# A hybrid attention and convolution block: x's first half loaded ahead of the modulation weights, zero products at the start, one store on another queue

## The chip, the cores and the metric

One Trainium2 chip, of which the kernel uses one core. The metric is the device time of one execution in microseconds (us); the time of a kernel is the median of its runs.

## What is computed

The reference, cut to the parts that the changed stage works on:

```python
def rmsnorm(x, g):                       # over the 1024 features
    y = x * lax.rsqrt(jnp.mean(x * x, axis=-1, keepdims=True) + 1e-6)
    return y * g

def adaln(cond, w_ada, b_ada):           # w_ada: 1024 x 3072
    return jnp.split(jax.nn.silu(cond) @ w_ada + b_ada, 3, axis=-1)

def hybrid_layer(x, ctx, c, c_ctx, ...):
    shift, scale, gate = adaln(c, w_ada, b_ada)
    shift_c, scale_c, gate_c = adaln(c_ctx, w_ada, b_ada)
    h = rmsnorm(x, norm_g) * (1 + scale[:, None]) + shift[:, None]
    hc = rmsnorm(ctx, norm_g) * (1 + scale_c) + shift_c
    q, k, v, za, u, bg, cg, zc = jnp.split(h @ w_in, SPLIT_POINTS, axis=-1)
    ...                                  # QK-norm, axial rope on q and k, windowed attention with
                                         # a bias table and context keys; gated short convolution
    return x + gate[:, None] * (jnp.concatenate([attn, conv], axis=-1) @ w_out)
```

`x` is 1024 tokens by 1024 features, `ctx` is 256 tokens, `w_in` is 1024 x 4096, all in float32. The conditioning vectors `c` and `c_ctx` give a shift and a scale per feature; they come out of a product of two rows with `w_ada`.

## The kernel before

Large products are made with three TensorE passes each: an operand is split into a high part (float32r) and a rest, and high x high, high x rest and rest x high are added up (`mm3`, and written out in `first_columns`).

The stage that the diff touches is the first one. It makes `h` transposed, feature tile by feature tile: `hh[k]` and `hl[k]` are the high part and the rest of 128 features by 1024 tokens. At the same time it uses each feature tile at once for the first convolution group: three blocks of 128 columns of `w_in` (a chunk, `chunks[k]`) times `hh[k]` and `hl[k]`, added up over the eight feature tiles in six PSUM banks `acc0[u][half]` (`first_columns(half, k, part)`, where a part is one of the three passes: part 0 needs the chunk's high part `wh`, part 1 its rest `wl`, part 2 the rest of `h`). A half is 512 tokens, four tiles of 128: `xx[0]` to `xx[3]` and `xx[4]` to `xx[7]`.

The steps for a tile of x: `square` (ScalarE, with the sum over the row), `root` (VectorE adds the epsilon, GpSimd takes the power -0.5 of the 128 sums), `norm` (VectorE scales the tile in place). Then for a half and a feature tile: `transposed` (TensorE, four transposes into a PSUM bank) and `turn`: ScalarE writes the modulated high part `h`, VectorE or ScalarE the full value `hw`, VectorE the rest of `h`.

The steps for the shifts and scales: slabs of `w_ada` are loaded, 256 columns for the shift (`j = 0`) and 256 for the scale (`j = 1`), so that pair `m` serves the feature tiles `2m` and `2m + 1`. `products(m, j)` multiplies the two activated conditioning vectors (two columns of weights) with the slab over eight tiles of 128 rows, in plain float32 for `m < 2`, where every product leaves two matmul records in the trace. `row_copy` brings the result rows to SBUF, and `modulation` turns them by tiny products into a column per feature tile, which VectorE completes in `ab`. From `m = 2` on the slab is split into `slabh` and `slabl` first.

In the trace the PSUM tile of slabs and transposes is called `tr`, that of `first_columns` `acc`, a tile of x `xx`, its sums `xss`, a chunk `wr` (`wh` and `wl` when split). Nearly all instructions have line 55, since the wrapper class `ordered` records them.

The order of the work is written out by hand. While `strict` holds the engines, each instruction of TensorE, ScalarE, VectorE and GpSimd is tied behind the one before it in program order, and the loads that SP issues too. A DMA that another engine than SP issues isn't tied. So an engine that waits holds up all that is written behind it, and so does SP: a load whose buffer isn't free yet, or a store whose data isn't ready, keeps all later transfers waiting.

The order of the loads before: both slabs of pair 0 (in two parts of 512 KB each), four tiles of x, a chunk, four tiles of x, a chunk, and then the slabs and chunks that follow as buffers come free (slabs of pairs 1 to 3 share three buffers, chunks five). Later, in the loop over `m` from 1 to 3, GpSimd makes the rope tables `rg` in `gains`, and SP stores them to `rope_d`, from where the next stage loads them; behind this store SP issues the chunks of the next column group (`chunk_load(CQ, k)`), then the small copies that build the bias tables (`bias_tables`, `t_d` in the trace), and then the first loads of the next stage (`uraw`, a unit of weights for the convolution and gates). The next stage makes q, k and v tile by tile (`pacc`): ScalarE and VectorE normalize and rotate a tile (`qn`, `rot`), and TensorE transposes it (`trA`, `trB`). All four engines go on through attention and the output projection, which the diff doesn't touch.

Of the kernel before, what the change touches and what calls it, by code (L numbers as in the profile page):

```python
# [19 lines left out]
P = 128  # L20
# [19 lines left out]
def body(tc, es, x, ctxt, w_ada, b_ada, w_in, q_g, k_g, rpbr, w_out, vecs, cst, out):  # L40
# [100 lines left out]
    def place(k, shape, dtype, name):  # L141

        return hpool.tile(shape, dtype, name=name, tag=f"h{k}")
# [383 lines left out]
    def load_x(ts):  # L527
        for t in ts:
            xx[t] = xp.tile([P, D], F32, name="xx", tag="xx", bufs=8)
            sp.dma_start(xx[t], x[0, t * P:(t + 1) * P])  # L530

    def load_slab(m, j):

        new = place(6 + j, [P, KT, 256], F32, "slab") if m == 0 else sl.tile([P, KT, 256], F32, name="slab", tag="slab", bufs=3)
        n = 2 if m == 0 else 1
        for i in range(n):
            rows = slice(KT // n * i, KT // n * (i + 1))
            sp.dma_start(new[:, rows], bass.AP(w_ada.tensor, w_ada.offset + j * D + 256 * m + 3 * D * P * rows.start,
                                               [[3 * D, P], [3 * D * P, KT // n], [1, 256]]))
        slabs[m, j] = new  # L540

    def load_chunks(ks):
        for k in ks:
            chunks[k] = chunk_load(CU, k)

    load_slab(0, 0)
    load_slab(0, 1)
    load_x(range(4))
    load_chunks([0])
    load_x(range(4, 8))  # L550
    load_chunks([1])
    load_slab(1, 0)
    load_slab(1, 1)
    load_chunks([2, 3])
# [3 lines left out]
    for u, half in (0, 0), (2, 0), (0, 1), (2, 1), (1, 0), (1, 1):  # L558
        acc0[u][half] = ps0.tile([P, 512], F32, name=f"acc{u}{half}", tag=f"acc{u}{half}")

    pv = tr()
    pe.transpose(pv[:, :nvec], vec[:nvec], ident[:nvec, :nvec])
    dve.tensor_copy(vecT, pv[:, :nvec])
    act.activation(c2[:].rearrange("p k a -> p a k"), vecT[:, 0:16].rearrange("p (a k) -> p a k", a=2), AF.Silu)
    dve.tensor_scalar(b1, bsc, 1.0, None, ALU.add)
    c4 = cp.tile([P, KT, 4], F32R, name="c4")
    act.copy(c4[:, :, 0:2], c2)
    dve.tensor_tensor(c4[:, :, 2:4], c2, c4[:, :, 0:2].bitcast(F32), ALU.subtract)

    sums = {}  # L570
# [34 lines left out]
    def row_copy(m):  # L605
        n = 2 if m < 2 else 4
        rw = cvp.tile([4, 512], F32, name="rw", tag="ub", bufs=2)
        act.copy(rw[:n], mods[m][:n])
        return rw[:n]

    def modulation(m, rw):

# [77 lines left out]
    def gains(tables):  # L690

        rw, gqk = tables
        pool.tensor_scalar(gqk[:, 0], gqk[:, 0], 0.125, None, ALU.mult)
        gkc1 = cp.tile([P, 1, HD], F32, name="gkc")
        pool.tensor_tensor(gkc1[:, 0], gqk[:, 0], gqk[:, 1], ALU.mult)
        rg = sl.tile([P, 2, NB, 2, HD], F32, name="rg", tag="slab", bufs=3)
        for n in range(2):
            rraw = rw[:, 512 * n:512 * n + 512].rearrange("p (b d) -> p b d", d=HD)
            for k in range(2):
                pool.tensor_tensor(rg[:, n, :, k], rraw, gqk[:, k:k + 1].broadcast_to([P, NB, HD]), ALU.mult)  # L700
        sp.dma_start(rope_d, rg[:].rearrange("p n b k d -> p (n b k d)"))
        return gkc1[:]

    def bias_tables():
# [10 lines left out]

    more_h(range(6))

    products(0, 0)
    products(0, 1)
    for t in range(4):  # L720
        square(xx[t], t)
    root(0)
    root(1)
    norm(xx[0], 0)
    root(2)
    norm(xx[1], 1)
    root(3)
    norm(xx[2], 2)
    rw = row_copy(0)
    modulation(0, rw)  # L730
    norm(xx[3], 3)
    transposed(0, 0)
    transposed(0, 1)
    square(xx[4], 4)
    root(4)
    split_chunk(0)
    turn(0, 0, dve)
    square(xx[5], 5)
    norm(xx[4], 4)
    root(5)  # L740
    turn(0, 1, dve)
    first_columns(0, 0)
    square(xx[6], 6)
    norm(xx[5], 5)
    root(6)
    square(xx[7], 7)
    norm(xx[6], 6)
    root(7)
    split_chunk(1)
    norm(xx[7], 7)  # L750
    first_columns(0, 1)
    products(1, 0, range(4))
    transposed(1, 0)
    turn(1, 0, act)
# [668 lines left out]
```

## Time and profile before

| | |
|---|---|
| median of 3 runs | 651.97 us (651.77 to 652.3) |
| the profiled execution | 651.68 us |
| its span, first to last instruction | 649.9 us |
| mean granted TensorE clock | 0.994 |
| TensorE busy with matmuls | 629.0 us (97%), 3469 |
| TensorE weight loads | 539.2 us (83%) |
| VectorE | 431.9 us (66%) |
| ScalarE | 322.6 us (50%) |
| GpSimd | 129.4 us (20%) |
| DMA | 125.46 MB, mean 193 GB/s |

PE is TensorE, PEld its weight loads, ACT is ScalarE, DVE is VectorE, POOL is GpSimd, SP is SyncE, which issues most transfers; PEq, SPq and the like are an engine's own queue of instructions. A line of the timeline has the start, the length, the engine, the source line, the operation with the tiles that it writes and reads and its shape, the count of merged instructions, and in brackets the idle time ahead of it with what ended that. Lengths of matmuls are modelled and overlap; the distance from one start to the next is the better measure. A line of the windows has the stretch, its length, the busy time and count of TensorE, its weight loads, VectorE, ScalarE and GpSimd, then the granted clock, the DMA engines' share and GB/s.

### The profile page before, as it was taken

The numbers are of one execution on the slowest core, as the hardware profiler recorded it, in microseconds if no ns is written. First come the engines' busy times: TensorE is split into PE (matmuls) and PEld (weight loads), VectorE is DVE, ScalarE is ACT, GpSimd is POOL, SyncE is SP. The second block draws the span as 40 slices with busy tenths as digits, with TensorE's granted clock in tenths as the row PEclk, the third lists the DMA queues.
The fourth block names the chain that finished last, engine by engine and source line by source line (L and its number), as shares of the span: only waits on it lengthen the run. The fifth ranks groups of instructions, "written<-read, shape, count | busy, mean of one in ns | idle before, by whom it ended". The sixth has DMA issues, their size and how long they took to land.

```text
span 649.9 us, 10273 instructions
## 1 busy us (share of the span) xinstructions
PE 629.0 (97%) x3469; PEld 539.2 (83%) x3469; DVE 431.9 (66%) x814; ACT 322.6 (50%) x693; POOL 129.4 (20%) x137
## 2 busy tenths in 40 slices
PE   5799999999999999999999999999999999999997
PEld 1467799899899999977877888888888888888885
DVE  1557774966684856457786889988998864575111
ACT  3466653442553635428677558565685645352000
POOL 1203203312222132101121111111211111004321
PEclk9799999999999999999999999999999999999999
DMA  8854637686686898789939576886782223966521
GB/s 321 314 179 166 168 105 243 202 263 196 196 278 177 251 262 254 187 228 218 241 103 238 145 179 191 211 213 153 207 190 75 74 75 118 324 222 222 178 102 50
DMA packets 118864, 125.46 MB, mean 193 GB/s; under 512 B 32817, under 2 KB 89353, under 8 KB 117532
## 3 DMA queue, kind: packets, MB, share of 16 engines
q1 hardware_dynamic: 112348, 113.23, 60.9%
q10 hardware_dynamic: 6208, 11.05, 5.3%
q0 software_dynamic: 256, 0.54, 0.3%
q8 instruction: 27, 0.44, 0.3%
q14 instruction: 25, 0.20, 0.1%
HBM read 88.01 MB, written 38.53 MB: 195 GB/s over the span
## 4 chain that ended last, share of the span: by engine, by line
PE 72%; DMA 7%; DVE 7%; ACT 5%; SPq 4%; issue 2%; POOL 1%; ACTq 0%; DVEq 0%; POOLq 0%
PE pu L55 22%; PE pacc L55 17%; PE po L55 5%; PE pout L74 4%; PE pout L75 4%; PE pout L76 4%; SPq L55 3%; PE tr L55 3%; PE cacc L55 3%; PE pss L55 2%; PE pmx L55 2%; DMA v<-v_d 2%; DMA k_s<-k_d 2%; PE pc L55 2%; DVE mx L55 2%
## 5 line engine op out<-in xcount | busy, mean ns | idle before, releaser
L55 PE MATMUL pu<-h,uh 128*128 128x512 f32 x544 | 169.0, 392 | 0.0
L55 PE MATMUL pacc<-wh,h 128*128 128x384 f32 x512 | 135.1, 338 | 0.0
L55 PEld LDWEIGHTS pu<-h,uh 128*128 128x128 f32 x544 | 98.2, 188 | 17.0
L55 PE MATMUL pu<-h,ul 128*128 128x512 f32 x272 | 106.3, 391 | 0.0
L55 PEld LDWEIGHTS pacc<-wh,h 128*128 128x128 f32 x512 | 92.9, 188 | 0.1
L55 POOL TENSOR_TENSOR plc<-sc,phc 128x512 fp32r<-128x512 f32 x32 | 42.5, 1328 | 221.9 <-ACT sc L55 113.2
L55 PE MATMUL pacc<-wl,h 128*128 128x384 f32 x256 | 85.6, 335 | 0.0
L55 POOL TENSOR_TENSOR ss<-ss,few 128x4 f32<-128x4 f32 (+1 forms) x40 | 42.0, 1051 | 126.9 <-DVE ss L55 126.5
L55 PEld LDWEIGHTS pu<-h,ul 128*128 128x128 f32 x272 | 51.1, 188 | 11.2
L55 DVE TENSOR_TENSOR mx<-mx,sb 128x384 f32<-128x384 f32 (+1 forms) x64 | 55.1, 869 | 2.0
L75 PE MATMUL pout<-wol,yh 128*128 128x512 f32 x128 | 49.8, 389 | 0.0
L76 PE MATMUL pout<-woh,yl 128*128 128x512 f32 x128 | 49.6, 389 | 0.0
L74 PE MATMUL pout<-woh,yh 128*128 128x512 f32 x128 | 48.3, 389 | 0.0
L55 PEld LDWEIGHTS pacc<-wl,h 128*128 128x128 f32 x256 | 48.1, 188 | 0.1
L55 DVE TENSOR_REDUCE ss<-sq 128x4 f32<-128x260 f32 (+1 forms) x40 | 15.7, 393 | 46.0 <-ACT sq L55 45.0
L55 ACT COPY mg<-pmx 128x256 f32<-128x256 f32 x32 | 12.0, 374 | 57.8 <-PE pmx L55 47.2
L55 ACT ACTIVATE sq<-pacc 128x256 f32<-128x256 f32 x32 | 12.3, 386 | 53.1 <-PE pacc L55 52.3
L1355 DVE TENSOR_TENSOR ot<-pout,gate 128x512 f32<-128x512 f32 x16 | 10.8, 688 | 40.2 <-PE pout L76 37.7
L55 DVE TENSOR_TENSOR pll<-sb,phl 128x768 fp32r<-128x768 f32 (+2 forms) x33 | 29.3, 889 | 7.9 <-ACT sb L55 7.9
L1356 POOL TENSOR_TENSOR ot<-ot,xr 128x512 f32<-128x512 f32 x15 | 19.6, 1315 | 68.6 <-DVE ot L1355 67.6
L55 DVE TENSOR_TENSOR sc<-sc,mg 128x512 f32<-128x512 f32 x32 | 21.8, 683 | 17.1 <-ACT mg L55 17.1
L55 ACT ACTIVATE qn<-pacc,ss 128x64 f32<-128x64 f32 x128 | 30.1, 330 | 6.0 <-POOL ss L55 3.2
(146 smaller groups left out, 1276.0 us busy)
## 6 DMA issues: line engine op xcount, KB each, us to landing
uraw<-in_w_in SPq DMA_DIRECT2D x34, 256.0 KB
q_d<-qs SPq DMA_DIRECT2D x64, 128.0 KB
k_s<-k_d SPq DMA_DIRECT2D x16, 512.0 KB
q_s<-q_d SPq DMA_DIRECT2D x32, 256.0 KB
wr<-in_w_in SPq DMA_DIRECT2D x40, 192.0 KB
slab<-in_w_ada SPq DMA_DIRECT2D x6, 1024.0 KB
t_d<-btw SPq DMA_DIRECT2D x8, 576.0 KB
bt<-t_d SPq DMA_DIRECT2D x8, 576.0 KB
```

The source lines that it names most:

```text
L55: i = emit(*a, **kw)
L74: i = pe.matmul(ps, ah, bh, start=first, stop=False)
L75: pe.matmul(ps, ah, bl, start=False, stop=False)
L76: pe.matmul(ps, al, bh, start=False, stop=last)
L1355: dve.tensor_tensor(ot, ps, gate[:, cols], ALU.mult)
L1356: (dve if (nh, t) == (1, NB - 1) else pool).tensor_tensor(ot, ot, xr, ALU.add)
```

## The change

- The order of the loads: four tiles of x come first; then the weights of pair 0 as two slabs by feature tile (`load_first_slabs(k)`: 128 columns of the shift and 128 of the scale each, in the two places where the slabs of 256 columns were), with a chunk and two tiles of x in between.
- `products`, `row_copy` and `modulation` of pair 0 are done by feature tile: `first_products`, `first_row`, `first_modulation`, in two of the accumulators' banks that aren't in use yet. The vector transpose goes to such a bank as well.
- `keep_clock(n)` issues n bf16 products of 128 x 512 zeros into a bank that is overwritten later: 6 at the very start, 22 behind the vector transpose, 4 behind the first and the second tile of x, and 4 behind the first modulation.
- The order of the steps up to `products(1, 0)` is written anew: each of the first three tiles of x is squared, scaled and transposed by itself, for both feature tiles; `first_columns(0, 0)` is done in three parts between the products and the modulation of feature tile 1; `turn(0, 1)` and `split_chunk(1)` stand ahead of `root(4)`.
- The store of the rope tables is issued by GpSimd instead of SP.

```diff
@@ -531,24 +531,30 @@
 
     def load_slab(m, j):
 
-        new = place(6 + j, [P, KT, 256], F32, "slab") if m == 0 else sl.tile([P, KT, 256], F32, name="slab", tag="slab", bufs=3)
-        n = 2 if m == 0 else 1
-        for i in range(n):
-            rows = slice(KT // n * i, KT // n * (i + 1))
-            sp.dma_start(new[:, rows], bass.AP(w_ada.tensor, w_ada.offset + j * D + 256 * m + 3 * D * P * rows.start,
-                                               [[3 * D, P], [3 * D * P, KT // n], [1, 256]]))
+        new = sl.tile([P, KT, 256], F32, name="slab", tag="slab", bufs=3)
+        sp.dma_start(new, bass.AP(w_ada.tensor, w_ada.offset + j * D + 256 * m,
+                                  [[3 * D, P], [3 * D * P, KT], [1, 256]]))
         slabs[m, j] = new
+
+    def load_first_slabs(k):
+
+        both = place(6 + k, [P, 2, KT, P], F32, "slab")
+        for j in range(2):
+            sp.dma_start(both[:, j], bass.AP(w_ada.tensor, w_ada.offset + j * D + P * k,
+                                             [[3 * D, P], [3 * D * P, KT], [1, P]]))
+        slabs[k] = both
 
     def load_chunks(ks):
         for k in ks:
             chunks[k] = chunk_load(CU, k)
 
-    load_slab(0, 0)
-    load_slab(0, 1)
     load_x(range(4))
+    load_first_slabs(0)
     load_chunks([0])
-    load_x(range(4, 8))
+    load_first_slabs(1)
+    load_x([4, 5])
     load_chunks([1])
+    load_x([6, 7])
     load_slab(1, 0)
     load_slab(1, 1)
     load_chunks([2, 3])
@@ -558,13 +564,23 @@
     for u, half in (0, 0), (2, 0), (0, 1), (2, 1), (1, 0), (1, 1):
         acc0[u][half] = ps0.tile([P, 512], F32, name=f"acc{u}{half}", tag=f"acc{u}{half}")
 
-    pv = tr()
+    warm = cvp.tile([P, 512], BF16, name="warm", tag="ub", bufs=2)
+    pool.memset(warm, 0.0)
+
+    def keep_clock(n):
+
+        for _ in range(n):
+            pe.matmul(acc0[2][1], warm[:, :P], warm, start=True, stop=True)
+
+    keep_clock(6)
+    pv = acc0[0][1]
     pe.transpose(pv[:, :nvec], vec[:nvec], ident[:nvec, :nvec])
     dve.tensor_copy(vecT, pv[:, :nvec])
     act.activation(c2[:].rearrange("p k a -> p a k"), vecT[:, 0:16].rearrange("p (a k) -> p a k", a=2), AF.Silu)
     dve.tensor_scalar(b1, bsc, 1.0, None, ALU.add)
     c4 = cp.tile([P, KT, 4], F32R, name="c4")
     act.copy(c4[:, :, 0:2], c2)
+    keep_clock(22)
     dve.tensor_tensor(c4[:, :, 2:4], c2, c4[:, :, 0:2].bitcast(F32), ALU.subtract)
 
     sums = {}
@@ -607,6 +623,30 @@
         rw = cvp.tile([4, 512], F32, name="rw", tag="ub", bufs=2)
         act.copy(rw[:n], mods[m][:n])
         return rw[:n]
+
+    def first_products(k, j):
+
+        ps = mods[k] = acc0[1 - k][1]
+        for kt in range(KT):
+            pe.matmul(ps[:2, P * j:P * j + P], c2[:, kt], slabs[k][:, j, kt], start=(j == 0 and kt == 0),
+                      stop=(j == 1 and kt == KT - 1), skip_group_check=True)
+
+    def first_row(k):
+        rw = cvp.tile([4, 512], F32, name="rw", tag="ub", bufs=2)
+        act.copy(rw[:2, :256], mods[k][:2, :256])
+        return rw[:2]
+
+    def first_modulation(k, rw):
+
+        pm = mods.pop(k)
+        for j in range(2):
+            pe.matmul(pm[:, 2 * j:2 * j + 2], rw[:, P * j:P * j + P], comb[:2], start=(j == 0), stop=(j == 1),
+                      skip_group_check=True)
+        both = lambda v: v[:, k:k + 1].broadcast_to([P, 2])
+        abk = ab[:, k].rearrange("p (w j) -> p j w", j=2)
+        dve.tensor_tensor(abk[:, 0], pm[:, 0:2], both(bsh), ALU.add)
+        dve.tensor_tensor(abk[:, 1], pm[:, 2:4], both(b1), ALU.add)
+        dve.tensor_tensor(abk[:, 1], abk[:, 1], both(ng), ALU.mult)
 
     def modulation(m, rw):
 
@@ -698,7 +738,7 @@
             rraw = rw[:, 512 * n:512 * n + 512].rearrange("p (b d) -> p b d", d=HD)
             for k in range(2):
                 pool.tensor_tensor(rg[:, n, :, k], rraw, gqk[:, k:k + 1].broadcast_to([P, NB, HD]), ALU.mult)
-        sp.dma_start(rope_d, rg[:].rearrange("p n b k d -> p (n b k d)"))
+        pool.dma_start(rope_d, rg[:].rearrange("p n b k d -> p (n b k d)"))
         return gkc1[:]
 
     def bias_tables():
@@ -715,40 +755,48 @@
 
     more_h(range(6))
 
-    products(0, 0)
-    products(0, 1)
-    for t in range(4):
+    for t in range(3):
         square(xx[t], t)
-    root(0)
-    root(1)
-    norm(xx[0], 0)
-    root(2)
-    norm(xx[1], 1)
+        root(t)
+        norm(xx[t], t)
+        transposed(0, 0, [t])
+        transposed(0, 1, [t])
+        if t < 2:
+            keep_clock(4)
+    first_products(0, 0)
+    square(xx[3], 3)
     root(3)
-    norm(xx[2], 2)
-    rw = row_copy(0)
-    modulation(0, rw)
     norm(xx[3], 3)
-    transposed(0, 0)
-    transposed(0, 1)
+    transposed(0, 0, [3])
+    transposed(0, 1, [3])
+    first_products(0, 1)
+    rw = first_row(0)
+    first_modulation(0, rw)
+    split_chunk(0)
+    keep_clock(4)
+    turn(0, 0, dve)
+    first_products(1, 0)
+    first_columns(0, 0, (0,))
+    first_products(1, 1)
+    rw = first_row(1)
     square(xx[4], 4)
+    first_columns(0, 0, (1,))
+    first_modulation(1, rw)
+    first_columns(0, 0, (2,))
+    turn(0, 1, dve)
+    split_chunk(1)
     root(4)
-    split_chunk(0)
-    turn(0, 0, dve)
     square(xx[5], 5)
     norm(xx[4], 4)
     root(5)
-    turn(0, 1, dve)
-    first_columns(0, 0)
     square(xx[6], 6)
     norm(xx[5], 5)
     root(6)
+    first_columns(0, 1)
     square(xx[7], 7)
     norm(xx[6], 6)
     root(7)
-    split_chunk(1)
     norm(xx[7], 7)
-    first_columns(0, 1)
     products(1, 0, range(4))
     transposed(1, 0)
     turn(1, 0, act)
```

## The prediction

> **What bounds the kernel now.** I read the page first, then the first 75 us engine by engine in the timeline, then the windows of two microseconds for the granted clock, then the waits of SP's own queue, and last TensorE's waits behind 30 us.
>
> The page says that TensorE is the bound:
>
> ```profile
> span 649.9 us, 10273 instructions
> ...
> PE 629.0 (97%) x3469; PEld 539.2 (83%) x3469; DVE 431.9 (66%) x814; ACT 322.6 (50%) x693; POOL 129.4 (20%) x137
> ```
>
> Only 21 us of the span are without a matmul, so a change to the order of the start can win or lose a few microseconds. TensorE's timeline of the start shows where (start, length, operation, count, idle before it and what ended that):
>
> ```profile
> 6.02 9.03 PE L55 MATMUL tr<-slab,c 128*2 128x256 f32 x32 [2.44 <-DMA slab<-in_w_ada]
> 16.81 1.05 PE L55 MATMUL tr<-ci,rw 2*128 2x2 f32 x8 [1.76 <-ACT rw L55]
> ...
> 19.12 0.77 PE L55 MATMUL tr<-ci,xx 128*128 128x128 f32 x5 [0.79 <-DVE xss L55]
> 20.32 1.65 PE L55 MATMUL acc<-h,wh 128*128 128x512 f32 x3 [0.43 <-ACT h L55]
> ...
> 26.80 1.42 PE L55 MATMUL acc<-h,wl 128*128 128x512 f32 x3 [1.18 <-DVE wl L55]
> 28.02 1.48 PE L55 MATMUL acc<-h,wh 128*128 128x512 f32 x3
> 29.43 2.40 PE L55 MATMUL tr<-slab,c 128*2 128x256 f32 x8
> 31.76 0.66 PE L55 MATMUL tr<-ci,xx 128*128 128x128 f32 x4
> 32.35 1.89 PE L55 MATMUL tr<-slab,c 128*2 128x256 f32 x8
> ...
> 47.64 1.10 PE L55 MATMUL tr<-slabh,c 128*4 128x256 f32 x8 [0.35 <-ACT hw L55]
> ...
> 49.51 0.85 PE L55 MATMUL acc<-h,wh 128*128 128x512 f32 x3
> 50.20 0.84 PE L55 MATMUL acc<-h,wl 128*128 128x512 f32 x3
> ```
>
> From 28.02 on TensorE hardly waits: its one idle stretch ahead of 50 us is the 0.35 at 47.64. The change leaves TensorE's order from `products(1, 0)` on as it was. So one moment measures the whole front: the end of `transposed(1, 0)`, the first transposes of x's second half, at 32.35 now. I call it R. What moves R moves the end, unless TensorE waits later.
>
> Such a wait stands further on. SP's order, the ScalarE instructions that wait for it, and TensorE:
>
> ```profile
> SPq L55 <- POOL rg L55: 13.1, 1, 13.1
> ```
>
> ```profile
> 67.31 0.33 SPq L55 DMA_DIRECT2D rope_d<-rg  x1
> 67.68 9.45 SPq L55 DMA_DIRECT2D wr<-in_w_in  x8
> 77.18 5.45 SPq L55 DMA_DIRECT2D t_d<-in_rpb  x8
> ...
> 96.73 0.93 SPq L55 DMA_DIRECT2D uraw<-in_w_in  x2
> ```
>
> ```profile
> 72.96 1.06 ACT L55 CAST wh<-wr 128x384 fp32r<-128x384 f32 x2 [2.09 <-DMA wr<-in_w_in]
> ...
> 103.14 0.62 ACT L55 CAST uh<-uraw 128x512 fp32r<-128x512 f32 x1 [11.78 <-DMA uraw<-in_w_in]
> ```
>
> ```profile
> 114.23 0.33 PE L55 MATMUL trA<-ci,rot 128*128 128x128 f32 x1 [0.87 <-DVE rot L55]
> ```
>
> SP stands 13.1 us before the rope store, until GpSimd has made `rg`. Behind it queue the chunks of the next group, for which ScalarE waits 2.09; behind those the bias tables, which take SP until 96; and behind those `uraw`, for which ScalarE waits 11.78. ScalarE, VectorE and GpSimd come late to the first projected tiles, and TensorE idles 0.87.
>
> **Part one: x ahead of the slabs.** The first 512 KB of the list is now x0 instead of half a slab, so it lands at about 5.9, where TensorE began on the slab (6.02). The steps from there, by rows of ScalarE and VectorE:
>
> ```profile
> 11.33 1.06 ACT L55 ACTIVATE sqj<-xx 128x1024 bf16<-128x1024 f32 x1 [7.01 <-DMA xx<-in_x]
> ...
> 12.69 1.06 ACT L55 ACTIVATE sqj<-xx 128x1024 bf16<-128x1024 f32 x1 [0.21 <-DMA xx<-in_x]
> ...
> 16.20 0.56 ACT L55 COPY rw<-tr 2x512 f32<-2x512 f32 x1
> ...
> 19.49 0.78 ACT L55 ACTIVATE h<-tr,ab 128x512 fp32r<-128x512 f32 x1 [0.92 <-PE tr L55]
> ```
>
> ```profile
> 12.51 0.15 DVE L55 TENSOR_SCALAR xss<-xss 128x1 f32<-128x1 f32 x1 [7.99 <-ACT sqj L55]
> ...
> 18.31 0.75 DVE L55 TENSOR_SCALAR xx<-xx,xss 128x1024 f32<-128x1024 f32 x1
> ...
> 20.30 0.81 DVE L55 TENSOR_SCALAR hw<-tr,ab 128x512 f32<-128x512 f32 x1 [0.71 <-ACT h L55]
> 21.14 0.69 DVE L55 TENSOR_TENSOR h<-hw,h 128x512 fp32r<-128x512 f32 x1
> ...
> 24.59 0.14 DVE L55 TENSOR_SCALAR xss<-xss 128x1 f32<-128x1 f32 x1
> 25.46 0.75 DVE L55 TENSOR_SCALAR xx<-xx,xss 128x1024 f32<-128x1024 f32 x1 [0.73 <-POOL xss L55]
> 26.13 0.15 DVE L55 TENSOR_SCALAR xss<-xss 128x1 f32<-128x1 f32 x1
> 26.20 0.55 DVE L55 TENSOR_TENSOR wl<-wr,wh 128x384 fp32r<-128x384 f32 x1
> ```
>
> Square to VectorE's add 1.18 (11.33 to 12.51); add to scaling, by way of GpSimd's power, 0.87 (24.59 to 25.46); scaling to the next tile's add 0.67 (25.46 to 26.13); scaling to TensorE's transpose 0.81 (18.31 to 19.12). In the new order VectorE has add and scaling of one tile directly behind each other, with nothing between that covers GpSimd, so a tile costs 0.87 + 0.67 = 1.54. That is more than the spacing of the landings (11.33 to 12.69, 1.36). The tiles are ready for TensorE at 8.8, 10.3, 11.8 and 13.4.
>
> The slabs by feature tile are four transfers of 512 KB behind x3. At 1.36 each the first two land at about 11.3 and 12.7 and, one chunk later, the others at 14.5 and 15.9. Their runs are halved; at twice that spacing they would still come about when TensorE asks (below), so they cost nothing.
>
> **Part two: TensorE up to the second modulation.** Zero products first: six, the vector transpose, 22 more. One costs 0.23 at the full clock (49.51 to 50.20 for three) and 0.41 to 0.47 at the slow one (26.80 to 28.02 to 29.43). The six take 2.6 slow; if a start near 1.6 (an estimate) has them over by 4.2, five more slow and 17 fast end at 10.3, which holds up x0 by 1.5; two batches of four between the x tiles add 0.9 each. So x2's transposes end at 13.0 if the zeros bind, at 12.1 if x2 does. From there, at the lower end: products of feature tile 0, 16 records of half the old width, by the row with the same streaming time (47.64 to 49.51, 1.87), 14.0; two transposes of x3 at 0.15 (31.76 to 32.35 for four), 14.3; products 16.2; row copy 0.6 (16.20 to 16.81), 16.8; half of the eight combining records of 1.05, 17.3; four zeros, 18.2; products 20.1; three accumulations 20.8; products 22.6. At the upper end 23.6. I take 23.1. In the old order the first modulation began at 16.81; the front has gained nothing by here, since both feature tiles' products now lie behind x.
>
> **Part three: x's second half, the price of the change.** ScalarE's list now has `first_row(1)` ahead of `square(xx[4])`, so ScalarE stands idle for these products although x4 has landed. VectorE's list has both turns and the chunk's split ahead of `root(4)`, and then four tiles at 1.54 without cover; in the old order these scalings lie between other work and are over by 28. From 23.1: copy 0.5, square 1.2, modulated `h` 0.8 (19.49 to 20.30), `hw` 0.85 (20.30 to 21.14), `h`'s rest 0.65, `wl` 0.5, 0.1 of hand-over: `root(4)` at 27.7. Then 0.87 + 3 x 1.54 to x7's scaling at 33.2, 0.81 to TensorE, 0.15 for one transpose: **R = 34.15**, 1.8 later than 32.35. Bounds by the two ends above: 1.3 and 2.3. TensorE's own work isn't late: `first_columns(0, 1)` ends at about 29.3 (29.43 now), four products at 31.1, and then it waits for x7. The zeros keep the clock up in a stretch which isn't the one that ends last.
>
> **Part four: the rope store.** SP no longer waits for `rg`. Three of the next chunks have free buffers, land early, and ScalarE loses its 2.09 wait. In this stretch TensorE was fed, so that itself is worth nothing; but the last chunk load, the bias tables and `uraw` come earlier by up to 2.09 (I take 1.3, because the ScalarE instruction behind these casts then waits for TensorE's transposes). That closes the 0.87 before 114.23: 0.9 gained, with bounds 0 and 1.0. GpSimd pays for the issue:
>
> ```profile
> 551.82 2.08 POOL L507 DMA_DIRECT2D rb<-ri_d  x4 [3.15 <-ACT yh L1332]
> ```
>
> 0.52 for one. Behind it on GpSimd are the context's two powers, and VectorE's scaling of `xc` for them; TensorE asks for `xc` only in the loop's last turn, so nothing to 0.5, taken as nothing.
>
> The Trainium skill (DMA: Bandwidth & Descriptors, Rules for kernel authors) speaks against this part: spreading transfers over issuing engines brings no bandwidth, as all share the same DMA engines, and only saves issue time. By that rule alone the 0.9 would be missing. The 13.1 us row shows a third thing, a queue held up by one wait.
>
> **Sum:** +1.8 - 0.9 = +0.9. The profiled execution took 651.68 (1.78 more than its span), so 652.6 for it; against the median of the runs, 651.97, which is 0.3 higher, 652.9. About 0.2% (1.3 us) is what a measurement of this kernel can tell from no change, so this counts as the same.
>
> **The rivals.** *The clock falls while TensorE waits for x7 (slower).* The clock column (before DMA share and GB/s) of the windows:
>
> ```profile
> 24.00:26.00 2.00, 1.17 (x4) 0.49 (x3) 1.27 (x4) 0.59 (x3) 0.55 (x1) 1.00 1.10 375
> 26.00:28.00 2.00, 1.20 (x3) 0.96 (x4) 1.50 (x4) 0.00 (x0) 0.73 (x1) 0.77 1.11 373
> 28.00:30.00 2.00, 2.00 (x6) 0.88 (x5) 0.00 (x0) 0.00 (x0) 0.00 (x0) 0.50 0.77 272
> 30.00:32.00 2.00, 2.00 (x10) 0.71 (x8) 0.00 (x0) 0.00 (x0) 0.00 (x0) 0.87 0.01 3
> ```
>
> If it is either whole or half, it was half for 0.92 + 2.0 + 0.52 = 3.4 us, directly after four microseconds in which TensorE was busy just over half. At half speed 3.4 us cost 1.7. From 31.1 to 34.1 TensorE has three transposes to do; if most of that falls into one such stretch, the slow clock follows: +0.9 + 1.7, **654.6**. If the stretch divides it, nothing. The Trainium skill (TensorE: Matmul & The Clock Gate, Part 1) has free-running windows of about 3.4 us and a slow clock after at least one idle window; the length agrees. By its word a wait of 3.0 would not do it, where the trace shows a half-busy stretch enough. Chance 0.16.
>
> *The rope store brings nothing*, because another wait holds the bias tables or `uraw`: **653.8**. For it: SP also waits for buffers there. Against: the chain ScalarE, VectorE, TensorE above. Chance 0.14.
>
> *x's second half is covered after all (faster).* If the scalings ran as closely as in the old order, x7 would be ready before TensorE's four products end at 31.1, R would be 31.7, and with the rope's 0.9 the sum -1.55: **650.4**. It decides if x7's scaling starts by 30.3. Against it: the written order of VectorE's list. Chance 0.16.
>
> *The zeros don't raise the clock (they do not do what they are there for).* All 30 at 0.45 delay x2's transposes to 18.7 and R by about 6 more: **659**. Against it: the products at 6.02 had two columns of weights and still 32 of them took only 9.03, under 0.41 each. Chance 0.04.
>
> **How the numbers follow.** Forecast 0.50: of it 0.40 within 0.2%, 0.08 slower, 0.02 faster, by the bounds of parts two to four. Clock 0.16 slower; rope 0.11 slower, 0.03 same; covered 0.13 faster, 0.03 same; zeros 0.04 slower. Together faster 0.15, same 0.46, slower 0.39. The range goes from the covered case, 650.3, to the clock case with the upper bound of part two, 655.6; it leaves out the zeros' case and the outer parts of both, under 0.2.
>
> **What would show it.** Right: transposes of x0 near 10, products by feature tile right behind x2, `square` of x4 not before 23, VectorE's adds 1.5 apart, an idle of 2 to 3 us that ends on VectorE's `xx` before `transposed(1, 0)`, no 13.1 row on SP, no idle before `trA`. Wrong: R ahead of 32.35, an idle before `trA` as before, or slow matmuls up to 14.

## The result, and the profile after

| | before | changed |
|---|---|---|
| median of 11 runs each | 651.34 us (648.23 to 653.66) | 654.86 us (652.6 to 657.19) |
| ratio, 95% interval | | 1.0063 (1.0045 to 1.0082) |
| the profiled execution | 651.68 us | 653.71 us |
| its span | 649.9 us | 651.9 us |

The changed kernel is slower by 0.63%, some 4 us (2.9 to 5.3 by the interval). The forecast was 652.9, +0.9, with a range to 655.6; so the sign was right, the time lies in the range, and the size was too small. The two profiled executions differ by 2.0. So there are two questions: did the front do what the prediction said, and where are the other microseconds?

The page of the changed kernel, its span and busy times:

```profile
span 651.9 us, 10425 instructions
...
PE 637.2 (98%) x3541; PEld 543.9 (83%) x3541; DVE 432.0 (66%) x817; ACT 322.8 (50%) x694; POOL 129.2 (20%) x139
```

TensorE has 72 matmuls more (40 zero products, and 32 because pair 0's products are done by feature tile) and is busy for 8.2 us more; VectorE, ScalarE and GpSimd have the work that they had. So what differs is the order, and the place to read it is the start. TensorE's timeline there, changed kernel (start, length, operation, count, idle before it and what ended that):

```profile
4.34 4.95 PE L55 MATMUL acc<-warm 128*128 128x512 bf16 x22
9.13 0.38 PE L55 MATMUL tr<-ci,xx 128*128 128x128 f32 x2
...
12.18 1.91 PE L55 MATMUL acc<-slab,c 128*2 128x128 f32 x16
...
22.82 0.98 PE L55 MATMUL acc<-h,wl 128*128 128x512 f32 x3
...
30.16 2.66 PE L55 MATMUL tr<-slab,c 128*2 128x256 f32 x8
32.74 0.55 PE L55 MATMUL tr<-ci,xx 128*128 128x128 f32 x3
33.94 0.33 PE L55 MATMUL tr<-ci,xx 128*128 128x128 f32 x1 [0.65 <-DVE xx L55]
34.20 1.89 PE L55 MATMUL tr<-slab,c 128*2 128x256 f32 x8
```

Read it from below. The first transposes of x's second half end at 34.20 (R), and the last idle time before that ends on VectorE's `xx`: x7's scaling is late. Further up, the products for feature tile 1 end at 22.82, and the zeros at 9.13. VectorE's and ScalarE's rows of the same stretch:

```profile
27.62 0.15 DVE L55 TENSOR_SCALAR xss<-xss 128x1 f32<-128x1 f32 x1
28.50 0.75 DVE L55 TENSOR_SCALAR xx<-xx,xss 128x1024 f32<-128x1024 f32 x1 [0.73 <-POOL xss L55]
29.16 0.15 DVE L55 TENSOR_SCALAR xss<-xss 128x1 f32<-128x1 f32 x1
...
33.13 0.75 DVE L55 TENSOR_SCALAR xx<-xx,xss 128x1024 f32<-128x1024 f32 x1 [0.73 <-POOL xss L55]
```

```profile
22.98 0.36 ACT L55 COPY rw<-acc 2x256 f32<-2x256 f32 x1 [4.28 <-PE acc L55]
23.25 1.05 ACT L55 ACTIVATE sqj<-xx 128x1024 bf16<-128x1024 f32 x1
```

Add to add is 1.54 (27.62 to 29.16), each scaling waits 0.73 for GpSimd, and ScalarE stood 4.28 for TensorE's products before it squared x4. The clock (the column before DMA share and GB/s) in the windows of two microseconds:

```profile
28.00:30.00 2.00, 2.00 (x6) 1.22 (x5) 0.82 (x2) 1.50 (x4) 1.00 (x2) 0.58 1.09 383
30.00:32.00 2.00, 2.00 (x6) 0.55 (x6) 1.23 (x3) 0.00 (x0) 0.56 (x2) 0.56 0.38 134
```

A slow stretch of 3.4 us lies here as it did before the change: it stretches four products from 1.89 to 2.66. But here it costs nothing, because the wait for x7 swallows it.

The rope store, on SP, on GpSimd and at TensorE's idle time behind it (rows of SP's, GpSimd's and TensorE's timeline):

```profile
97.18 0.96 SPq L55 DMA_DIRECT2D uraw<-in_w_in  x2
```

```profile
70.18 1.21 POOL L741 DMA_DIRECT2D rope_d<-rg  x1
```

```profile
115.41 0.33 PE L55 MATMUL trA<-ci,rot 128*128 128x128 f32 x1 [0.26 <-DVE rot L55]
```

The wait of 13.1 has left SP's queue. Counted from R, `uraw` is issued 1.4 earlier (96.73 - 32.35 = 64.38 before, 97.18 - 34.20 = 62.98 now), and the idle 0.87 is 0.26.

What lies behind? Three landmarks of TensorE in both kernels: the gate products, and the first and the last score product of the attention. First before, then changed:

```profile
171.99 1.88 PE L55 MATMUL pgate<-gacc,few 128*1 128x512 f32 x4
...
279.26 0.48 PE L55 MATMUL pss<-q_s,k_s 128*128 128x256 f32 x2
...
521.08 0.48 PE L55 MATMUL pss<-q_s,k_s 128*128 128x256 f32 x2
```

```profile
173.16 1.88 PE L55 MATMUL pgate<-gacc,few 128*1 128x512 f32 x4
...
280.44 0.48 PE L55 MATMUL pss<-q_s,k_s 128*128 128x256 f32 x2
...
523.00 0.48 PE L55 MATMUL pss<-q_s,k_s 128*128 128x256 f32 x2
```

Gate to attention is 107.27 before and 107.28 now. From the last score product to the last output product it is 123.96 in both (521.08 to 645.04, 523.00 to 646.96). Only the attention between them differs: 241.82 and 242.56. So the 2.0 between the two executions are R +1.85, R to gate -0.68 (139.64 to 138.96), attention +0.74. The first two are the prediction's +1.8 and -0.9; the third is not in it.

### The profile page after: what moved, and what is told of

It reads as the page before. It is cut to its first block, busy times and chain, and to the rows that moved or that the text cites. A ratio compares the mean times of both kernels' runs of the same rounds, so it can differ in the third digit from the quotient of the medians.

```text
span 651.9 us, 10425 instructions
## 1 busy us (share of the span) xinstructions
PE 637.2 (98%) x3541; PEld 543.9 (83%) x3541; DVE 432.0 (66%) x817; ACT 322.8 (50%) x694; POOL 129.2 (20%) x139
## 4 chain that ended last, share of the span: by engine, by line
PE 76%; DVE 7%; DMA 6%; ACT 4%; issue 1%; SPq 1%; ACTq 0%; DVEq 0%
PE pacc L55 20%; PE pu L55 20%; PE po L55 5%; PE pout L75 4%; PE pout L74 4%; PE pout L76 4%; PE cacc L55 4%; PE acc L55 3%; PE tr L55 3%; DMA v<-v_d 3%; DVE mx L55 2%; PE pss L55 2%; PE pmx L55 2%; PE pc L55 2%; DVE sb L55 1%; DMA k_s<-k_d 1%
```

## The experiments

Two things had to be told apart: which part of the change costs and which gains, and whether the forecast's reference (R = 32.35 in one execution of the kernel before) is typical. In the quoted expectations A is the prediction's mechanism (x7's uncovered scalings set R), B and C are as e1's expectation has them, and D is that a delay of the front grows on its way to the end. All profiles side by side; "idle" is TensorE's before that `trA` ("-" is under 0.15, which the timeline doesn't print), "gate" the first gate product, "attention" first to last score product, all in us. The ratio is to runs of the kernel before in the same measurement. e7 and e8 are a single run each and have none.

| kernel | R | idle | R to gate | attention | span | median | ratio (95%) |
|---|---|---|---|---|---|---|---|
| before | 32.35 | 0.87 | 139.6 | 241.8 | 649.9 | 651.34 | |
| e7, before again | 30.72 | 1.42 | 140.8 | 241.3 | 648.9 | 650.7 | |
| e5, before + delay | 32.60 | 1.40 | 140.9 | 241.2 | 651.5 | 653.22 | 1.0022 (0.9996 to 1.0047) |
| e2, store alone | 31.61 | - | 138.8 | 243.3 | 649.9 | 651.77 | 0.9994 (0.9969 to 1.0018) |
| e6, zeros in the old order | 30.98 | 0.27 | 139.0 | 242.1 | 648.9 | 650.41 | 0.9978 (0.9953 to 1.0002) |
| e9, and chunk earlier | 28.83 | - | 138.5 | 243.1 | 646.6 | 648.42 | 0.9951 (0.9927 to 0.9975) |
| e11, e9 with SP's store | 28.98 | 0.92 | 139.7 | 245.5 | 650.1 | 649.63 | 0.9960 (0.9936 to 0.9985) |
| changed | 34.20 | 0.26 | 139.0 | 242.6 | 651.9 | 654.86 | 1.0063 (1.0045 to 1.0082) |
| e8, changed again | 33.71 | 0.53 | 139.2 | 242.5 | 651.5 | 653.32 | |
| e10, changed, third time | 35.15 | - | 139.8 | 243.6 | 654.8 | 656.21 | 1.0081 (1.0048 to 1.0113) |
| e1, changed, SP's store | 34.20 | 0.62 | 139.4 | 247.0 | 656.6 | 657.64 | 1.0077 (1.0052 to 1.0102) |
| e3, scalings covered | 33.20 | 0.79 | 139.5 | 244.3 | 653.2 | 651.78 | 1.0011 (0.9987 to 1.0034) |
| e4, no zeros | 35.22 | - | 138.5 | 241.0 | 650.8 | 654.37 | 1.0054 (1.0032 to 1.0075) |
| e12, zeros in the wait | 33.82 | - | 138.5 | 245.7 | 654.1 | 655.65 | 1.0056 (1.0032 to 1.0080) |

### e1: the front alone

```diff
-        pool.dma_start(rope_d, rg[:].rearrange("p n b k d -> p (n b k d)"))
+        sp.dma_start(rope_d, rg[:].rearrange("p n b k d -> p (n b k d)"))
```

> The changed front, with the rope store back on SP's queue. Theory A (VectorE's uncovered scalings of x's second half set the end of the first transposes of that half, R; the store on GpSimd only returns something): R near 34.2 as in the changed kernel, SP again some 13 us before the store, and the idle before the first trA transposes back at about 0.9 instead of 0.3, so 0.6 slower than the changed kernel, 2 to 5 slower than before. Theory B (the store on GpSimd is what costs, by queueing in the next stage): within 1 us of before. Theory C (the slow clock makes what the medians have beyond the 2.0 of the two profiled spans): R the same, but the time depends on whether a slow stretch of 3.4 us lies in front of R (hidden by the wait for x7) or behind it (1.7 more).

SP's waits, then TensorE's timeline, then ScalarE's waits in the attention:

```profile
SPq L55 <- POOL rg L55: 13.2, 1, 13.2
```

```profile
115.83 0.33 PE L55 MATMUL trA<-ci,rot 128*128 128x128 f32 x1 [0.62 <-DVE rot L55]
```

```profile
ACT mg L55 <- DMA v<-v_d: 4.8, 1, 4.8
```

The 13.2 is back, and the idle time is 0.62, where 0.9 was expected. R is 34.20, the same as in the changed kernel, so the store doesn't touch R. From R to this product it takes 81.63 against 81.21 with the store on GpSimd: 0.4. The median is 2.8 above the changed kernel's, but the two intervals overlap by far. The long span comes from the attention: 247.0 here, where ScalarE waited 4.8 for a load of `v` that it waited 2.2 for in the kernel before.

### e2: the store alone

```diff
-        sp.dma_start(rope_d, rg[:].rearrange("p n b k d -> p (n b k d)"))
+        pool.dma_start(rope_d, rg[:].rearrange("p n b k d -> p (n b k d)"))
```

> The kernel before with only the rope store moved to GpSimd's queue. Theory A: R at 32.35 as before, the idle before trA down from 0.87 to 0.3 or less, 0.5 to 1.0 faster than before. Theory B: 1 to 3 slower than before, with new waits behind 110 us. Theory C says nothing of the store, but that the front's R moves by up to 1.7 from one profiled execution to the next with the place of the slow stretch.

```profile
112.69 0.33 PE L55 MATMUL trA<-ci,rot 128*128 128x128 f32 x1
```

The row of TensorE's timeline has no idle time before it any more. R to gate is 138.8, against 139.6 and 140.8 in the two profiles of the kernel before. The time is 0.9994 with an interval that holds 0.9969 to 1.0018: 0.9 us gained (0.14%) lies in it, and so does nothing. So the gain is shown at the place, not at the end.

### e3: the four scalings covered

Squares, adds and scalings of x4 and x5 go ahead of the second modulation, those of x6 and x7 between its steps:

```diff
     first_products(1, 1)
-    rw = first_row(1)
     square(xx[4], 4)
...
     root(4)
     square(xx[5], 5)
-    norm(xx[4], 4)
     root(5)
-    square(xx[6], 6)
+    norm(xx[4], 4)
     norm(xx[5], 5)
+    rw = first_row(1)
+    square(xx[6], 6)
...
+    turn(0, 1, dve)
+    split_chunk(1)
...
     root(7)
+    first_columns(0, 1)
     norm(xx[7], 7)
```

> The changed kernel with the scalings of x's second half covered: x4 and x5 are squared, summed and scaled ahead of the second row copy, while ScalarE and VectorE stand idle for TensorE, x6 behind the copy, x7 last. Theory A: x7's scaling starts by 30 instead of 33.1, R is set by TensorE's four products and comes to about 31.7 (32.7 if they fall into a slow stretch), 2 us ahead of the changed kernel's 34.2; the time 2 to 3 below the changed kernel and 0.5 to 1.5 below before. Rival: x's second half isn't what ends last, and the time stays within 0.7 of the changed kernel.

VectorE's and TensorE's timeline:

```profile
29.05 0.75 DVE L55 TENSOR_SCALAR xx<-xx,xss 128x1024 f32<-128x1024 f32 x1 [0.73 <-POOL xss L55]
```

```profile
30.14 2.54 PE L55 MATMUL tr<-slab,c 128*2 128x256 f32 x8
32.62 0.66 PE L55 MATMUL tr<-ci,xx 128*128 128x128 f32 x4
33.20 1.89 PE L55 MATMUL tr<-slab,c 128*2 128x256 f32 x8
```

x7's scaling starts at 29.05 instead of 33.13, and TensorE no longer waits for it: no idle time ahead of 32.62. The time goes from 1.0063 to 1.0011, 3.4 us back (by the two intervals, some 2 us either way). This is the experiment that carries the main point: the order of these steps, which leaves VectorE's scalings uncovered, was the price of the change. Two of the expected numbers were missed. R was to come to 31.7, or 32.7 with a slow stretch; in this execution it is only 1.0 earlier, at 33.20, since TensorE's own work now ends last and the slow stretch fell upon it (four products in 2.54 and not 1.89). An estimate of R without that stretch: in e7 the clock was whole there, and R came 4.00 after the products with `wl` began (26.72 to 30.72); these begin at 27.64 here, so 31.6. And the time was to be 0.5 to 1.5 below that of the kernel before, but it is 0.7 above it, and by the interval it may as well be equal. Freed of its price, the new front has an R near 31.6, and the old one has 31.3 (the mean of four profiles, under e7): by this it is no faster.

### e4: no zeros

```diff
-        for _ in range(n):
+        for _ in range(0):
             pe.matmul(acc0[2][1], warm[:, :P], warm, start=True, stop=True)
```

> The changed kernel without the zero products (all 36 left out). Theory A: the wait for x7 ends last either way; x0 to x3 aren't held up, the products by feature tile run partly at the slow clock (0.24 instead of 0.12 a record); R between 33.5 and 35, the time within 1 us of the changed kernel. Rival (the zeros are worth what the change put them in for): R later than 36 and the time 2 or more above the changed kernel. Other rival (the zeros on the path cost their length, 0.9 for the last four alone): 1 us faster.

TensorE's timeline:

```profile
11.88 3.57 PE L55 MATMUL acc<-slab,c 128*2 128x128 f32 x16
...
35.22 1.89 PE L55 MATMUL tr<-slab,c 128*2 128x256 f32 x8
```

Without the zeros the 16 products of the first feature tile take 3.57 and not 1.91, so the zeros do raise the clock. (The expectation says 36 zeros; the edit leaves out 40, 3541 - 3501 matmuls in the two pages.) R is 0.1 to 1.5 later than in the three profiles of the changed kernel. The times of the two can't be told apart (1.0054 and 1.0063): what the zeros bring at R doesn't pay for the new order.

### e5: a delay in the old order

Nine zero products (1.95 us) ahead of the second half of `products(1, 0)`, where the kernel before never waits:

```diff
     turn(1, 0, act)
+    keep_clock(9)
     products(1, 0, range(4, KT))
```

> The kernel before with nine zero products (1.95 us at the full clock) put between its first transposes of x's second half and the second part of products(1, 0), on TensorE alone: a delay of the size by which the change moved R. Theory A (what moves TensorE here moves the end by as much): 1.5 to 2.0 slower than before. Theory D (a delay grows in the next stages, as the first slow-down's medians were over twice the shift in the profiled front): 3 to 4.5 slower. Rival (a later wait absorbs it): within 0.5.

```profile
30.07 0.66 PE L55 MATMUL tr<-ci,xx 128*128 128x128 f32 x4
30.57 2.10 PE L55 MATMUL acc<-warm 128*128 128x512 bf16 x9
32.60 1.89 PE L55 MATMUL tr<-slab,c 128*2 128x256 f32 x8
```

This tests the rule on which the sum rests, that what moves R moves the end. 1.95 put in gave a ratio of 1.0022, 1.4 us, with an interval from -0.3 to +3.1. One to one fits, and a delay that grows to double does not. A delay that is absorbed would also lie in the interval; the profile speaks against it: R is 1.88 later than in e7, and the gate product is 1.94 later (173.45 and 171.51). The same rows hold a surprise: without the zeros R would have been near 30.66 here, and not 32.35.

### e7 and e8: both kernels profiled again

Nothing is edited in either.

> The kernel before, profiled once more for the place of the slow stretch. Theory C: R anywhere between 30.6 and 32.4, earlier than 32.35 where no slow stretch lies between 26 and 31 us; the length from the first scores of the attention to the last is near 242, whatever R is. Theory D: that length grows with R.

> The changed kernel, profiled once more. Theory A: R at 34.2 again, within 0.3, wherever the slow stretch lies, since x7's scaling ends last. Theory C: if no slow stretch lies before R, one may lie behind it, and the last products ahead of first_columns(1, 0) end 1 to 1.7 later than 40.15.

TensorE's timeline, first the kernel before, then the changed one:

```profile
28.31 1.89 PE L55 MATMUL tr<-slab,c 128*2 128x256 f32 x8
...
30.72 1.89 PE L55 MATMUL tr<-slab,c 128*2 128x256 f32 x8
...
113.80 0.33 PE L55 MATMUL trA<-ci,rot 128*128 128x128 f32 x1 [1.42 <-DVE rot L55]
```

```profile
33.45 0.33 PE L55 MATMUL tr<-ci,xx 128*128 128x128 f32 x1 [1.21 <-DVE xx L55]
33.71 1.89 PE L55 MATMUL tr<-slab,c 128*2 128x256 f32 x8
```

The old order has R = 30.72 here: the four products ahead of it take 1.89, where they took 2.40 in the profile that the prediction read. Four profiles of the old front have 32.35, 30.72, 31.61 (e2) and 30.66 (e5, before its zeros), mean 31.3. The changed front can't use a free clock in this stretch, because it waits for x7: in e8 the four products are over early, the wait before x7's transpose is 1.21 in place of 0.65, and R is 33.71 (34.2, within 0.3, was expected). Its four (with e10 and e1) are 34.20, 33.71, 35.15 and 34.20, mean 34.3. So the shift is 3.0 and not 1.8.

### e10: the changed kernel a third time

> The changed kernel against the kernel before a second time. By the profiles (R 34.2 and 33.7 against 32.35 and 30.7; the two gate products 1.2 to 1.4 later; the spans 2.0 to 2.6 apart): 2 to 3 slower. If the attention is longer behind the changed front, as the first comparison's 3.5 of the medians could mean: 3.5 to 5 slower again, and more than 243 from the first scores to the last.

TensorE's timeline and the windows:

```profile
34.74 0.47 PE L55 MATMUL tr<-ci,xx 128*128 128x128 f32 x1 [1.21 <-DVE xx L55]
35.15 3.28 PE L55 MATMUL tr<-slab,c 128*2 128x256 f32 x8
```

```profile
32.00:34.00 2.00, 0.75 (x4) 0.32 (x3) 0.88 (x3) 0.00 (x0) 0.91 (x2) 1.00 0.01 4
34.00:36.00 2.00, 1.25 (x4) 0.43 (x5) 0.69 (x1) 0.74 (x2) 0.00 (x0) 0.65 0.00 0
36.00:38.00 2.00, 2.00 (x6) 0.59 (x5) 1.16 (x2) 1.10 (x3) 0.00 (x0) 0.50 0.00 0
```

Here is the clock rival, which the prediction gave a chance of 0.16. TensorE works 0.75 of two microseconds while it waits for x6 and x7; then the clock is half for 1.4 + 2.0 = 3.4 us, and the eight products behind R take 3.28 and not 1.89. It costs 1.4, against the 1.7 foreseen, on top of R = 35.15. Of the two expected cases the larger came: 1.0081 is 5.3 us (3.1 to 7.4), with an attention of 243.6. In e8, in e1 and in the first profile these products take 1.89: it is one execution in four of this front. The zeros at the start also end later here, at 10.53 and not 9.13, and with them R.

### e6 and e9: the old order, made faster

e6 keeps the old order of loads, puts the store on GpSimd, and zeros into the gaps where TensorE waits:

```diff
     products(0, 1)
+    keep_clock(7)
...
-    transposed(0, 0)
-    transposed(0, 1)
+    for ts in (range(3), [3]):
+        transposed(0, 0, ts)
+        transposed(0, 1, ts)
+        keep_clock(2 if ts == [3] else 1)
...
     first_columns(0, 0)
+    keep_clock(7)
...
-    first_columns(0, 1)
+    first_columns(0, 1, (0,))
+    keep_clock(5)
+    first_columns(0, 1, (1, 2))
```

> The kernel before with the store of the rope tables on GpSimd's queue and 24 zero products in the gaps that TensorE has between 15 and 27 us, the order of everything else kept (the transposes of x3 behind those of the other tiles). Theory C (the old front's R depends on the clock: 32.35 in the profiled execution with a slow stretch from 27.1 to 30.5, near 30.6 without): granted clock 1.00 from 16 to 34 us, R at 30.6 to 31.0, the split chunk's wait still there; 1.5 to 2.5 faster than before with what the store brings. Rival (the clock is not what R hangs on): R at 31.6 to 32.4 and no more than 1 faster.

```profile
30.98 1.89 PE L55 MATMUL tr<-slab,c 128*2 128x256 f32 x8
```

The clock is whole from 14 to 46, and R is 30.98. But this is within the 30.7 to 32.4 that the old front gives anyway: the chunk's rest, and not the clock, now ends last. The ratio, 0.9978, can't quite be told from 1. So e9 moves the second chunk ahead of x6 and x7, and its split ahead of their scalings:

```diff
-    load_x(range(4, 8))
+    load_x([4, 5])
     load_chunks([1])
+    load_x([6, 7])
...
     first_columns(0, 0)
-    keep_clock(7)
+    split_chunk(1)
     square(xx[6], 6)
-    norm(xx[5], 5)
     root(6)
+    norm(xx[5], 5)
     square(xx[7], 7)
-    norm(xx[6], 6)
     root(7)
-    split_chunk(1)
+    norm(xx[6], 6)
     norm(xx[7], 7)
...
-    keep_clock(5)
+    keep_clock(4)
```

> The warm old front with the next wait behind it taken away: chunk 1 is loaded between x5 and x6 and split ahead of the squares of x6 and x7, which are summed ahead of the scalings of x5 and x6 on VectorE; fewer zeros, since the gap is shorter. Theory A (R is set by whatever comes last into first_columns(0, 1) and the first products, here the chunk's rest and no longer x7): R near 28.5 against 30.98 with the warm front alone, the distance from R to the gate row's products 139 us as in all kernels with the store on GpSimd, 2 to 3 faster than the warm front, 3 to 5 faster than before. Rival (the load of the next slab ends last): R stays above 30.

```profile
28.83 1.89 PE L55 MATMUL tr<-slab,c 128*2 128x256 f32 x8
```

R is 28.83, 2.5 ahead of the old front's mean, and the time 0.9951 (0.9927 to 0.9975): 3.2 us faster than the kernel before, and faster than both kernels. Note what it has in common with the change: the load order x4, x5, chunk, x6, x7. It lacks the slabs behind x and the uncovered scalings.

### e11: e9 with the store on SP

```diff
-        pool.dma_start(rope_d, rg[:].rearrange("p n b k d -> p (n b k d)"))
+        sp.dma_start(rope_d, rg[:].rearrange("p n b k d -> p (n b k d)"))
```

> The warm front with the early chunk, with the rope store back on SP's queue. If the store on GpSimd is worth more the earlier the front is (the gate row's products came 138.5 us after R with it, 139.4 to 140.8 with SP's store): the idle before the second trA back at 1 us or more, the gate products 1 to 2 later, 1 to 2 slower than the early chunk with the store on GpSimd, 1.5 to 2.5 faster than before. Rival (what it gains there is lost behind the gate products, where the kernels with the store on GpSimd took 477.1 to 480.6 us to the end and most of those with SP's 477.4 to 478.1): no slower than the early chunk.

```profile
110.91 0.33 PE L55 MATMUL trA<-ci,rot 128*128 128x128 f32 x1 [0.92 <-DVE rot L55]
```

The idle time is back at 0.92, and R to gate is 139.7 against 138.5. The times, 0.9960 and 0.9951, can't be told apart.

### e12: zeros in the wait for x7

```diff
-    transposed(1, 0)
+    for t in range(4):
+        transposed(1, 0, [t])
+        keep_clock((0, 4, 6, 0)[t])
```

> The changed kernel with ten zero products in TensorE's wait for x6 and x7 (four behind x5's transpose, six behind x6's). They end before x7 is ready, so R stays at 33.7 to 34.7; no slow stretch between 30 and 40 us, so the products behind R take 1.8 and not 3.2 as in the second measurement of the changed kernel. Theory (the slow clock behind R is part of what the medians have over the shift of R): 0.5 to 1.5 faster than the changed kernel, 2 to 3.5 slower than before. Rival (it is not): 3.5 to 5 slower than before, as the changed kernel.

```profile
32.19 1.46 PE L55 MATMUL acc<-warm 128*128 128x512 bf16 x6
...
33.82 1.89 PE L55 MATMUL tr<-slab,c 128*2 128x256 f32 x8
```

TensorE is busy up to x7's transpose, and the products behind R take 1.89. But R is still x7's, and the time is 1.0056. It was expected 2 to 3.5 above the kernel before if the slow clock had a share in the medians, and 3.5 to 5 if not; it is 3.7, with an interval (2.1 to 5.2) that holds both. What the clock rival costs on average, 0.35 if it comes in one execution of four, is less than these runs can tell. So that rival is shown to exist (e10), and its share of the median is not measured.

## Why the prediction was right or wrong

**The front's own times: right.** The zeros were over at 9.13, 1.2 earlier than put (10.3; in the third profile of the changed kernel 10.5), so that x2 and not the zeros ended last there. Behind that each step came within 0.3 of its place: the second modulation's products at 22.82 (23.1, with 22.6 to 23.6 as bounds), `root(4)` at 27.62 (27.7), 1.54 a tile, x7's scaling at 33.13 (33.2), R at 34.20 (34.15). That it comes from VectorE's uncovered list is shown by e3, which moves only the squares, adds and scalings of x4 to x7 and gets 3.4 us back. Two of the signs came out weaker than foretold. The idle time that ends on `xx`, 2 to 3, was 0.65 in the first profile, where the slow clock stretched the products ahead of it, and 2.0 in two parts in e8 and e10 (0.8 before x6's transpose, 1.2 before x7's). And some idle time before `trA` was left: 0.26, 0.53 and, in e10, none.

**The term that was mis-sized: R +1.8.** It measured +3.0. The minuend was right, the subtrahend was not: 32.35 came from one execution, in which a slow stretch of the clock (27.1 to 30.5) lay on TensorE's path. In three other profiles of the old front R was 30.7 to 31.6. The prediction used these very windows, for a rival, and didn't ask what R would be without that stretch. The two fronts aren't alike in this: the old one is held by TensorE's own work and gains when the clock is free, the new one is held by x7 and can't.

**The range: in part luck that the time lies in it.** The forecast's own terms with their bounds (R +1.3 to +2.3, store 0 to -1.0) reach from 652.3 to 654.3, and the measured 654.86 lies above them. It lies in the range only because the range was drawn up to the clock case, which came in one profile of four. The upper end is also 0.5 too high for its own working: the clock case, 654.6, with part two's bound of 0.5 is 655.1, and not 655.6; 654.86 lies inside that as well.

**The rope store: right in place and cause, and in size on the mean.** With SP's store TensorE idles 0.87, 1.42, 1.40, 0.62 and 0.92, mean 1.05, in five profiles; in the nine with GpSimd's none in five and 0.26, 0.27, 0.53 and 0.79 in the others, mean 0.21. That is 0.84 less, where 0.9 was forecast. R to gate has means of 140.1 and 138.8 (e10 counted without its 1.4), 1.3 less. Single profiles overlap: e3, with GpSimd's store, idles 0.79, and e1, with SP's, 0.62. The pairs that differ in the store alone have R to gate apart by 0.8 and 2.0 (e2 against the two of the kernel before), 1.2 (e9, e11) and 0.2 to 0.9 (e1 against the three of the changed kernel). The prediction left open whether the Trainium skill's rule that another issuing engine brings no bandwidth (DMA: Bandwidth & Descriptors, Rules for kernel authors) would leave the term at nothing. At this place the trace shows a gain, and its cause is the wait that left SP's queue. In the end time it could not be seen by itself (e2).

**The clock rival: right as a mechanism, wrong as an alternative.** It was weighed as something that either happens to this kernel or not. It happens in some executions and not in others, so it is a term of the sum: 1.4 in one of four. The Trainium skill (TensorE: Matmul & The Clock Gate, Part 1) has the clock fall after an idle window. No idle time ahead of the slow stretch of e10 is longer than 1.21 us; as in the kernel before, a half-busy stretch was enough. The windows tell a little of why one execution falls and another does not. In the 3.4 us just ahead of the fall TensorE was busy 1.79 in the kernel before (23.7 to 27.1), 1.83 in the changed one (24.9 to 28.3) and 1.58 in e10 (31.2 to 34.6). In e7 the same waits are parted otherwise, 2.23 and 2.28 of 3.4 (22.2 to 25.6 and 25.6 to 29.0), and the clock stayed whole. No threshold follows from these few: from 13.4 to 16.9 the kernel before was busy 1.65 of 3.4, and the clock stayed whole up to 20.

**The rivals that fell.** x's second half covered: no, 0.73 of wait on each scaling. Zeros that don't raise the clock: no, 1.91 with them and 3.57 without for the same 16 products (e4).

**What the prediction hadn't at all: the attention.** In the three profiles of the changed kernel it takes 242.6, 242.5 and 243.6, in the two of the kernel before 241.8 and 241.3: 1.4 more on the mean. Half of this lies at one place, near two thirds of it, where ScalarE's queue issues two stores. ScalarE's timeline, before and changed:

```profile
443.38 0.20 ACTq L1023 DMA_DIRECT2D rs_d<-ob  x1
...
444.69 0.37 ACT L55 COPY mg<-pmx 128x256 f32<-128x256 f32 x1 [2.71 <-PE pss L55]
```

```profile
445.76 0.20 ACTq L1071 DMA_DIRECT2D rs_d<-ob  x1
...
447.01 0.37 ACT L55 COPY mg<-pmx 128x256 f32<-128x256 f32 x1 [3.79 <-DMA rs_d<-ob]
```

The copy, for which VectorE's chain waits, comes behind the two stores in ScalarE's order. It starts 2.3 later in the span and 1.1 later counted from the first score product. From the first score product of one unit to that of the next, this turn of the loop takes 8.1 to 8.5 us in all six profiles that have the changed front with its zeros, 7.5 to 7.6 in the others, and 7.9 in e5. Why a change at the start is felt 400 us later was not tried and stays open; it is a pattern seen in the traces, and no experiment aimed at it. The rest of the attention's differences (241.0 to 247.0 over all profiles) lies mostly in three other turns of its loop and follows no part of the change. The longest are e1, e12 and e11, and these are also the only three in which the clock was half for a while inside the attention (from 333, 391 and 326 on, for 3.4 us each): after a long wait there, the next turn took 8.4 to 8.8 and not 7.2. The 1.4 itself is not shown to be the change's work, since the old front with the store on GpSimd has 242.1 to 243.3 too (e2, e6, e9).

**The sum as it stands:** R +3.0, clock behind R +0.35 (1.4 in one of four), R to gate -1.3, attention +1.4, together +3.5. The ratio gives 2.9 to 5.3. Without the attention's 1.4 the sum is +2.1, below that interval. So the sign and the largest term are shown, and 1 to 3 us of the time stay open.

## What to carry to other kernels

Profile the kernel before more than once when a slow clock can lie on its path: a moment read from one execution was 1 us off the mean of four here, more than the net effect of +0.9 that was forecast. When two engines hand a small value back and forth per tile, keep other work of the same list between the hand-overs: the same four scalings cost 3.4 us without cover (some 2 us either way). And zero products help little in a gap that doesn't end last: in e6 they made the clock whole and R stayed within the old front's spread, while an earlier load and an earlier split (e9) moved R by 2.

## What was not expected of the hardware

- Long stretches repeat within hundredths (gate to attention takes 107.27 or 107.28 in all fourteen profiles), and a few short ones differ by 1 to 2 us, where the clock or a load comes in.
- The clock was half for about 3.4 us in both places that were worked out: 28.3 to 31.8 in the changed kernel, 34.6 to 38.0 in e10. By the windows of e2 and e5 it was twice that there, 6.8: 18.9 to 25.8 and 17.1 to 23.9. No wholly idle stretch of that length came before either: in e10 TensorE was busy 0.75 of the two microseconds ahead.
- Zero products of bf16 count as work for the clock: with 36 of them ahead, the products by feature tile take 1.91 for 16, against 3.57 without.
- GpSimd took 1.21 us to issue the rope store. The prediction read 0.52 from another transfer.
